# A hybrid attention, retention and expert layer on one core: stored operand loaded earlier, one interleave re-weighted, gate tiles double-buffered

## The chip, the cores and the metric

The kernel runs on 1 core of one Trainium2 chip. The metric is device time in microseconds; lower is better. Engines are named as the profile names them: PE (matrix multiply), PEld (its weight load), DVE (vector), ACT (activation), POOL (here it only issues indirect gathers) and SP (it issues the other DMAs).

## The reference

One decoder layer on 1024 tokens of width 1024, with 16 meta tokens ahead of them:

```
hn = rmsnorm(h);  z = hn @ w_in
y_a = attention(z) @ w_mla_out          # 8 heads, causal, low-rank q and kv
y_r = retention(z) @ w_ret_out          # 8 heads, chunks of 128, group norm, silu gate
h  += (sigmoid(za) * y_a + sigmoid(zr) * y_r) @ w_mix_out
x   = rmsnorm(h);  q = x @ w_peer_q     # 8 heads
top-16 of 128 keys on each of two sides -> top-16 of the 256 pairs, softmax gates
out = h + sum over the 128 chosen experts of gate * gelu(x . peer_u[e]) * peer_v[e]
```

There are 16384 experts. All is float32; the kernel makes its large products from three products of a high and a low part.

## The kernel before

**Token groups.** The 8 blocks of 128 tokens form three groups: blocks 0 to 2, 3 and 4, and 5 to 7. Each group passes through `latents`, `mix` (retention and attention), `merge` and `output`. `interleave(parts, counts)` steps two generators so that each reaches its count at the same time. `STEPS[1]` holds the counts for the merge of group n beside the latents of group n+1: (112, 90) for the second merge and the third latents. A merge has 112 steps: per column block two products of 4 + 2 and 4 + 4 steps. The third latents, counted through the yields of the code, have 98. What is left of one part when the other is done runs alone.

**Two ways for the experts.** Group 0 gathers its chosen rows (`gathered`, a background task: POOL gathers a row, DVE multiplies it at L1082 or adds it at L1087, 2 x 128 rows a block). The other five blocks (640 tokens) go through all experts densely in `dense`: 128 expert rows `e`, each with 128 experts. For each `e`, `scores(e)` loads 512 KB of `peer_ut` into a `raw` tile (ring of 3), splits it on ACT (`whi`) and DVE (`wlo`), multiplies it with the 256 stored tokens of group 1 (`x_hi`, `x_lo`) and the 384 of group 2 (`xT_hi`, `xT_lo`), and applies gelu into `gl`.

**The stored operand.** Group 1's normed tokens are written to DRAM (`xT_d`) by its `output`. At the start of `dense` they are loaded back through four `raw` tiles and copied by ACT into `x_hi` and `x_lo` (L1142), behind everything of the last `output`.

**Order in `dense`.** First 48 expert rows are scored and parked in DRAM (`gl_d`) while the gate matrix is built in the background: 20 stores of 2 MB into `gate_d`. Then `finish(0)`, five loads of `y`, and 16 groups of 8 expert rows, in the order `es`. A group is two quads of four rows; a quad is either parked (its `gl` comes back by a DMA of 320 KB, without PE work) or scored anew. Eight groups are scored then parked, four are scored twice, four parked then scored (these are the 4th, 8th, 12th and 16th). For each row `weights(e)` multiplies `gl` with its gates from the tile `gt` on DVE (L1209), and splits the product into `c_hi` (ACT) and `c_lo` (DVE). Then PE multiplies the eight products with `peer_vt` into `zacc`, in two halves, and DVE adds them to `y` (L1242).

**The gate tile.** `gt` holds the gates of one quad: one DMA of 1280 KB at every fourth row (L1208), into a pool with `GTB = 1` buffer:

```
if e % 4 == 0:
    gt[0] = vp.tile([P, nt, 4, TS], F32, name="gt", bufs=GTB)
    nc.sync.dma_start(gt[0], gate_d[...])
V.tensor_tensor(gl, gt[0][:, :, e % 4], gl, OP.mult)
```

Each load can start only when the multiplications of the quad before have read the buffer.

**What sets the order.** Each engine, and each DMA queue, takes its instructions in a fixed order that the tile framework makes from the program; a waiting instruction holds those behind it. Buffers are rings: a tile waits for the last reader of the tile whose place it takes. Background gathers are paced by the weight pieces that the main work consumes.

Of the kernel before, what the change touches and what calls it, by code (L numbers as in the profile page):

```python
# [12 lines left out]
F32 = mybir.dt.float32  # L13
# [29 lines left out]
RING = 3  # L43
ROWS = 4
SPLIT = 3
GTB = 1
DELAY = 8.0
STEPS = (((86, 72), (116, 64), (116, 144)), ((112, 90), (112, 90), (112,)), (80, 50))
HEAD = 20
BUBBLE = 12  # L50
LEAVE = ((6, 6, 3), (0, 1, 1))
# [92 lines left out]
def hybrid_layer(ctx: ExitStack, tc: tile.TileContext, out, a, dbg=None):  # L144
# [7 lines left out]
    ps = ctx.enter_context(tc.tile_pool(name="ps", bufs=2, space=PSUM))  # L152
    dram = ctx.enter_context(tc.tile_pool(name="dram", bufs=1, space=DRAM))

    gat = ctx.enter_context(tc.tile_pool(name="gat", bufs=1, side="right"))


# [90 lines left out]
        T.matmul(o, st[1], mv[0], start=False, stop=last)  # L248

    def square_sum(src, acc):  # L250
        junk = work.tile([P, TW], F32, name="zt").bitcast(BF16)
        S.activation(junk[:, :src.shape[-1]], src, AF.Square, accum_out=acc)

    def norm_scale(tiles, name):
# [61 lines left out]
    def group(g):  # L316
# [273 lines left out]
        def retention(hp):  # L590
# [45 lines left out]
            def add_state(i):  # L636
                pst = tr()
                for s in range(2):
                    T.matmul(pst[64 * s:64 * s + 64, 0:P], qn[:, i, 128 + 64 * s:128 + 64 * s + 64],
                             vr[:, i, P * s:P * s + P], start=True, stop=True)  # L640
                new = work.tile([P, P], F32, name=f"state{hp}")
                if hp in state:
                    V.tensor_tensor(new, pst[:, 0:P], state[hp], OP.add)
                else:
                    V.tensor_copy(new, pst[:, 0:P])
                state[hp] = new
# [179 lines left out]
        def merge():  # L826
            mg = own.mg
            for c in range(KD):
                for s, src in enumerate((own.oTs, own.yTs)):
                    pz = zacc()  # L830
                    for j, w in enumerate(split_pieces(a["w_z"][2 * c + s], KD, P)):
                        mm3(pz[:, 0, :W], w, [t[:, j, :W] for t in own.hn], j == 0, j == KD - 1)
                        if j % 2:
                            yield
                    n = len(src)
                    for j, w in enumerate(split_pieces(a["w_ret" if s else "w_mla"][c], n, P)):
                        mm3(pz[:, 1, :W], w, src[j], j == 0, j == n - 1)
                        if j % 2:
                            yield
                    th = work.tile([P, TW], F32, name="zt")[:, :W]  # L840
                    S.activation(th, pz[:, 0, :W], AF.Tanh, scale=0.5)
                    V.scalar_tensor_tensor(th if s else mg[:, c], th, 1.0, pz[:, 1, :W], op0=OP.add, op1=OP.mult)
                    if s:
                        V.tensor_tensor(mg[:, c], mg[:, c], th, OP.add)


        def output():
# [20 lines left out]
            if not last:  # L868
                if g >= NGROUP:
                    ktp = ctx.enter_context(tc.tile_pool(name=f"kt{g}", bufs=1, side="right", reuse_waits="tile"))  # L870
                fcs, fc = pool("fc", "right")
                scs = [pool(f"sc{i}_", "right") for i in reversed(range(nbk))][::-1]
            xps, xp = pool("xp", "right")
            xT = [xp.tile([P, KD, W], F32R, name=n) for n in ("xT_hi", "xT_lo")]
            hps, hp_ = pool("h2", "right")
# [215 lines left out]
        nc.sync.dma_start(out[P * b:P * b + P], acc[0])  # L1091


    def gate_matrix(i, kt, gT, p):

        stage = {}

        def products(t8, pairs):
            t0 = t8 // TS * TS
            if t8 == t0:  # L1100
                stage[0] = p.tile([P, P, TS], F32, name="stage", bufs=2)
            pg = zacc()
            oa, ob = pairs
            for t in range(8):
                T.matmul(pg[:, t // 4, P * (t % 4):P * (t % 4) + P], oa[:, t // 2, :, t % 2], ob[:, t // 2, :, t % 2],
                         start=True, stop=True)
            S.activation(stage[0][:, :, t8 - t0:t8 - t0 + 8].rearrange("p e (q t) -> p e q t", q=2),
                         pg.rearrange("p q (t e) -> p e q t", t=4), AF.Copy)
            if t8 == t0 + TS - 8:
                nc.sync.dma_start(gate_d[(P * i + t0) // TS], stage[0].rearrange("p e t -> p (e t)"))  # L1110

        pending = None
        for t8 in range(0, P, 8):
            at = lambda t: t.rearrange("p (q r) -> p q r", r=2).unsqueeze(2).to_broadcast([P, 4, P, 2])
            eq = [p.tile([P, 4, P, 2], BF16, name=f"eq{n}", bufs=2) for n in range(2)]
            for n in range(2):
                V.tensor_tensor(eq[n], iota_2.unsqueeze(1).to_broadcast([P, 4, P, 2]), at(kt[:, n, t8:t8 + 8]), OP.is_equal)
            pairs = [p.tile([P, 4, P, 2], F32, name=n, bufs=2) for n in ("oa", "ob")]
            S.activation(pairs[0], eq[0], AF.Copy)
            V.tensor_tensor(pairs[1], eq[1], at(gT[:, t8:t8 + 8]), OP.mult)  # L1120
            if pending:
                products(*pending)
            pending = (t8, pairs)
            yield 1.7
        products(*pending)

    def dense(xT):
        nt = DT // TS
        pacing["rates"] = RATES[3]
        last = GROUPS[-1]  # L1130
        segments = [(xT, len(last) * P)]
        xdp = ctx.enter_context(tc.tile_pool(name="xd", bufs=1, side="right", reuse_waits="tile"))
        for g, blocks in enumerate(GROUPS[NGROUP:-1]):
            w = P * len(blocks)
            t = [xdp.tile([P, KD, w], F32R, name=f"x_{n}{g}") for n in ("hi", "lo")]
            per = 1024 // w
            for dst, src in zip(t, xT_d[g]):
                for j in range(0, KD, per):
                    n = min(per, KD - j)
                    raw = wp.tile([P, 1024], F32, name="raw", bufs=RING)  # L1140
                    nc.sync.dma_start(raw[:, :n * w].rearrange("p (j c) -> p j c", j=n), src[:, j:j + n])
                    S.activation(dst[:, j:j + n].rearrange("p j c -> p (j c)"), raw[:, :n * w], AF.Copy)  # L1142
            segments.insert(g, (t, w))
        starts = [sum(w for _, w in segments[:k]) for k in range(len(segments))]
        order = list(range(len(segments)))
        ups, up = ExitStack(), None
# [14 lines left out]
        def routes():  # L1161

            kts, ktp = open_pool("ktl", "right")
            fcs, fc = open_pool("fcd", "right")
            n = len(last)
            top = top_tiles(n, fc)
            for h in range(H):
                first_top16(h, top, key_scores(queries(h, xT, n, fc), n))
                yield 1.85 * n
            for i, b in enumerate(last):  # L1170
                found = yield from choose(b, *top[i], fc, ktp)
                routed.append(found)
            fcs.close()
            pacing["rates"] = RATES[4]
            gms, gm = open_pool("gm")
            for i, (kt, gT) in enumerate(routed):
                yield from gate_matrix(i, kt, gT, gm)
            gms.close()
            kts.close()

# [11 lines left out]
        for b in range(NGATH, NBLK):  # L1192
            ys.append(vp.tile([P, D], F32, name=f"y{b}"))
            nc.sync.dma_start(ys[-1], h2_d[b])
        gt = {}

        def activations(e):
            if e >= AHEAD:
# [5 lines left out]
        def weights(e, gl):  # L1204

            if e % 4 == 0:
                gt[0] = vp.tile([P, nt, 4, TS], F32, name="gt", bufs=GTB)
                nc.sync.dma_start(gt[0], gate_d[:, :, TS * e:TS * e + 4 * TS].rearrange("n p (e t) -> p n e t", e=4))  # L1208
            V.tensor_tensor(gl.rearrange("p (n t) -> p n t", t=TS), gt[0][:, :, e % 4],  # L1209
                            gl.rearrange("p (n t) -> p n t", t=TS), OP.mult)  # L1210
            hi = vp.tile([P, DT], F32R, name="c_hi", bufs=CB)
            lo = vp.tile([P, DT], F32R, name="c_lo", bufs=CB)
            split(hi, lo, gl)
            return hi, lo


        es = [4 * n + k for n in sorted(range(P // 4), key=lambda n: (n + 0.5) / AHEAD if 4 * n < AHEAD else
                                        (n + 0.5 - AHEAD / 4) / (P - AHEAD)) for k in range(4)]
        for e0 in range(0, P, GE):
            group = es[e0:e0 + GE]  # L1220
            ne = len(group)
# [43 lines left out]
    iota = load_const("iota", a["c_iota"], [P, P])  # L1265
    iota_i = const.tile([P, 16, 2 * H], BF16, name="iota_i")
    V.tensor_copy(iota_i, iota[:, 0:16].unsqueeze(2).to_broadcast([P, 16, 2 * H]))
    iota_2 = const.tile([P, P, 2], BF16, name="iota_2")
    V.tensor_copy(iota_2, iota.unsqueeze(2).to_broadcast([P, P, 2]))
    gqr = load_const("gqr", bcast(a["g_qk"], 32, 64), [P, 32])  # L1270
    gkr = load_const("gkr", bcast(a["g_qk"], 32, 96 + 64), [P, 32])
    gqk = const.tile([P, 2], F32, name="gqk")
# [16 lines left out]
    for n, now in enumerate(groups):  # L1289
# [4 lines left out]
        now.open_merge(following)  # L1294
        interleave([now.merge()] + ([following.latents()] if following else []), STEPS[1][n])
        rest = now.output()
    dense(rest)
    finish(1)

# [17 lines left out]
```

## Time and profile before

| | |
|---|---|
| median of 3 runs | 3574.49 us (3563.3 to 3585.4) |
| profiled execution | 3571.28 us, span 3569.5 us |
| PE busy | 3322.8 us (93%) |
| DVE busy | 2687.7 us (75%) |
| ACT busy | 1268.1 us (36%) |
| mean granted TensorE clock | 0.968 |
| DMA | 837.12 MB, mean 235 GB/s |

The span is that of the profiled execution; its own time is 1.78 us more, and 3.2 us under the median. In the time rows the profile gives start and duration in microseconds, then the engine, line and operation, and in brackets how long the engine sat idle before and what released it. The granted clock is a share of 2.4 GHz; it is 1.00 or 0.50 (1.2 GHz), and values between are means over a stretch.

### The profile page before, as it was taken

The page shows a single profiled execution, that of the slowest core. Times are in us where ns is not written, and L with a number is a line of the kernel's source. Part 1 is how long each engine was busy: PE and PEld are TensorE (multiplying, and loading weights), DVE is VectorE, ACT ScalarE, POOL GpSimd, SP SyncE. Part 2 cuts the span into 40 slices and gives each one's busy share as a digit, 9 for nine tenths or more (in the row PEclk, how much of TensorE's full clock was granted, in tenths as well). Part 3 has the DMA queues.
Part 4 walks back from the last instruction along what each step waited for, and adds up shares of the span by engine and source line. Part 5 has one row for each costly group of instructions (what it writes and reads, how often), then busy time and mean ns, then how long its engine had stood idle before and what let it go on. Part 6 is the DMA issues. An engine that isn't in the chain of part 4 may idle for free.

```text
span 3569.5 us, 53608 instructions
## 1 busy us (share of the span) xinstructions
PE 3322.8 (93%) x20376; PEld 3022.3 (85%) x20376; DVE 2687.7 (75%) x5659; ACT 1268.1 (36%) x2097; POOL 1090.4 (31%) x772
## 2 busy tenths in 40 slices
PE   8999989989789998999999799999999999999999
PEld 7888988788767898999999788888788778887788
DVE  5645469898796676798988578777778777877776
ACT  3445334544445533234566222222222222222221
POOL 0000000112011122013434445454445454554454
PEclk9999999999899999999999899999999999999999
DMA  3322353557654377456777888888889888988886
GB/s 129 121 78 94 133 193 113 167 201 253 215 156 139 135 239 254 152 177 238 284 289 295 305 289 305 306 308 301 287 284 321 288 291 290 322 307 288 286 300 246
DMA packets 329251, 837.12 MB, mean 235 GB/s; under 512 B 45713, under 2 KB 140689, under 8 KB 326177
## 3 DMA queue, kind: packets, MB, share of 16 engines
q1 hardware_dynamic: 218400, 431.00, 35.4%
q0 software_dynamic: 110592, 402.70, 32.0%
q8 instruction: 160, 2.62, 0.3%
q14 instruction: 99, 0.80, 0.1%
HBM read 755.16 MB, written 78.43 MB: 234 GB/s over the span
## 4 chain that ended last, share of the span: by engine, by line
PE 49%; issue 17%; DMA 13%; DVE 11%; POOL 6%; ACT 3%; POOLq 0%; SPq 0%; DVEq 0%; ACTq 0%
PE zacc L246 10%; PE zacc L248 10%; PE zacc L247 10%; DMA row<-in_peer_v_dram,eidx 7%; POOL row L1065 6%; PE tr L246 4%; PE tr L247 4%; PE tr L248 4%; DMA gt<-gate_d 3%; DVE wlo L219 2%; PE tr L765 2%; PE sc L729 1%; DVE acc L1087 1%; ACT whi L218 1%; DMA row<-in_peer_u_dram,eidx 1%
## 5 line engine op out<-in xcount | busy, mean ns | idle before, releaser
L1065 POOL DMA_INDIRECT row<-in_peer_u_dram,eidx x384 | 486.3, 1266 | 1731.5 <-DVE row L1082 839.9
L218 ACT ACTIVATE whi<-raw 128x1024 fp32r<-128x1024 f32 (+2 forms) x508 | 520.7, 1026 | 1274.3 <-PE zacc L248 643.5
L219 DVE TENSOR_TENSOR wlo<-raw,whi 128x1024 fp32r<-128x1024 f32 (+2 forms) x508 | 599.5, 1181 | 369.6 <-ACT whi L218 368.7
L1065 POOL DMA_INDIRECT row<-in_peer_v_dram,eidx x384 | 603.9, 1573 | 718.5 <-DVE acc L1087 605.4
L246 PE MATMUL zacc<-whi,c_hi 128*128 128x512 f32 x1280 | 509.1, 398 | 57.0 <-ACT c_hi L218 45.9
L1087 DVE SCALAR_TENSOR_TENSOR acc<-row,dots,acc 128x1024 f32<-128x1024 f32 x384 | 482.0, 1278 | 91.0 <-DMA row<-in_peer_v_dram,eidx 90.2
L248 PE MATMUL zacc<-whi,c_lo 128*128 128x512 f32 x1280 | 506.8, 396 | 2.9 <-DVE c_lo L219 2.9
L247 PE MATMUL zacc<-wlo,c_hi 128*128 128x512 f32 x1280 | 506.3, 396 | 0.0
L1082 DVE SCALAR_TENSOR_TENSOR row<-row,xn 128x1024 f32<-128x1024 f32 x384 | 463.2, 1218 | 54.7 <-DMA row<-in_peer_u_dram,eidx 54.3
L246 PE MATMUL tr<-xT_hi,whi 128*128 128x384 f32 (+1 forms) x1216 | 416.3, 342 | 40.5 <-ACT gl L1158 39.3
L247 PE MATMUL tr<-xT_lo,whi 128*128 128x384 f32 (+1 forms) x1216 | 411.9, 339 | 0.0
L248 PE MATMUL tr<-xT_hi,wlo 128*128 128x384 f32 (+1 forms) x1216 | 411.7, 339 | 0.0
L246 PEld LDWEIGHTS zacc<-whi,c_hi 128*128 128x128 f32 x1280 | 245.4, 192 | 115.2 <-ACT c_hi L218 49.3
L246 PE MATMUL tr<-x_hi,whi 128*128 128x256 f32 x1024 | 295.9, 289 | 12.7 <-ACT whi L218 10.2
L248 PEld LDWEIGHTS zacc<-whi,c_lo 128*128 128x128 f32 x1280 | 244.7, 191 | 60.0 <-DVE c_lo L219 8.6
L247 PE MATMUL tr<-x_lo,whi 128*128 128x256 f32 x1024 | 290.2, 283 | 0.0
L248 PE MATMUL tr<-x_hi,wlo 128*128 128x256 f32 x1024 | 290.1, 283 | 0.0
L247 PEld LDWEIGHTS zacc<-wlo,c_hi 128*128 128x128 f32 x1280 | 245.3, 192 | 50.7
L246 PEld LDWEIGHTS tr<-xT_hi,whi 128*128 128x128 f32 x1216 | 233.6, 192 | 43.2 <-ACT gl L1158 40.8
L246 PE MATMUL zacc<-whi,hn_hi 128*128 128x256 f32 x832 | 250.8, 301 | 3.8 <-ACT pT L780 1.3
L247 PE MATMUL zacc<-wlo,hn_hi 128*128 128x256 f32 x832 | 238.9, 287 | 1.4 <-DVE wlo L219 1.4
L248 PE MATMUL zacc<-whi,hn_lo 128*128 128x256 f32 x832 | 238.1, 286 | 0.0
(286 smaller groups left out, 6728.8 us busy)
## 6 DMA issues: line engine op xcount, KB each, us to landing
raw<-in_peer_ut_dram SPq DMA_DIRECT2D x128, 512.0 KB, 5.5
raw<-in_peer_vt_dram SPq DMA_DIRECT2D x128, 512.0 KB, 6.2
gate_d<-stage SPq DMA_DIRECT2D x20, 2048.0 KB, 9.1
gt<-gate_d SPq DMA_DIRECT2D x32, 1280.0 KB, 14.6
raw<-in_w_nat_dram SPq DMA_DIRECT2D x72, 512.0 KB, 3.5
raw<-in_w_z_dram SPq DMA_DIRECT2D x48, 512.0 KB, 3.3
gl_d<-gl SPq DMA_DIRECT2D x48, 320.0 KB, 2.9
gl<-gl_d SPq DMA_DIRECT2D x48, 320.0 KB, 6.4
```

The lines of the kernel that those rows point to most:

```text
L218: S.activation(hi, src, AF.Copy)
L219: V.tensor_tensor(lo, src, hi.bitcast(F32), OP.subtract)
L246: T.matmul(o, st[0], mv[0], start=first, stop=False)
L247: T.matmul(o, st[0], mv[1], start=False, stop=False)
L248: T.matmul(o, st[1], mv[0], start=False, stop=last)
L729: T.matmul(sc[:, c, 0:w], qh, kT[0:96, k0:k0 + w], start=True, stop=c < nch - 1)
L765: T.matmul(oo, vh[:, c + k], pT[:, k], start=False, stop=c + k == b)
L1065: G.indirect_dma_start(out=row, out_offset=None, in_=table, in_offset=bass.IndirectOffsetOnAxis(ap=eidx[:, k:k + 1], axis=0))
L1082: op = V.scalar_tensor_tensor(row, row, 1.0, xn, op0=OP.mult, op1=OP.mult, accum_out=dots[:, k:k + 1])
L1087: op = V.scalar_tensor_tensor(acc[k % 2], row, dots[:, k:k + 1], acc[k % 2], op0=OP.mult, op1=OP.add)
```

## The change

Four things. The stored operand is loaded and copied when the last group's `output` opens, ahead of its `w_mix` loads, by the new function `stored_tokens`, whose loop stood in `dense` before. The counts of the second merge beside the third latents become (112, 100). `gt` has two buffers; `gate_tile` issues the first load ahead of the group loop and each further one a quad ahead. To make room, `iota_2` moves from the constants into the gate-matrix pool, and the tiles `zt` and `state` into a pool `mw` that is closed ahead of `dense`.

```diff
-GTB = 1
+GTB = 2
-STEPS = (((86, 72), (116, 64), (116, 144)), ((112, 90), (112, 90), (112,)), (80, 50))
+STEPS = (((86, 72), (116, 64), (116, 144)), ((112, 90), (112, 100), (112,)), (80, 50))
...
+    mixers = ExitStack()
+    mw = mixers.enter_context(tc.tile_pool(name="mw", bufs=2))
...
-        junk = work.tile([P, TW], F32, name="zt").bitcast(BF16)
+        junk = mw.tile([P, TW], F32, name="zt").bitcast(BF16)
...
-                new = work.tile([P, P], F32, name=f"state{hp}")
+                new = mw.tile([P, P], F32, name=f"state{hp}")
...
-                    th = work.tile([P, TW], F32, name="zt")[:, :W]
+                    th = mw.tile([P, TW], F32, name="zt")[:, :W]
...
     def output():
...
+            if last:
+                segments.extend(stored_tokens())
             xps, xp = pool("xp", "right")
...
+    segments = []
+
+    def stored_tokens():
+        xdp = ctx.enter_context(tc.tile_pool(name="xd", bufs=1, side="right", reuse_waits="tile"))
+        for g, blocks in enumerate(GROUPS[NGROUP:-1]):
+            w = P * len(blocks)
+            t = [xdp.tile([P, KD, w], F32R, name=f"x_{n}{g}") for n in ("hi", "lo")]
+            per = 1024 // w
+            for dst, src in zip(t, xT_d[g]):
+                for j in range(0, KD, per):
+                    n = min(per, KD - j)
+                    raw = wp.tile([P, 1024], F32, name="raw", bufs=RING)
+                    nc.sync.dma_start(raw[:, :n * w].rearrange("p (j c) -> p j c", j=n), src[:, j:j + n])
+                    S.activation(dst[:, j:j + n].rearrange("p j c -> p (j c)"), raw[:, :n * w], AF.Copy)
+            yield t, w
...
     def dense(xT):
-        segments = [(xT, len(last) * P)]
...
-            segments.insert(g, (t, w))
+        segments.append((xT, len(last) * P))
...
             gms, gm = open_pool("gm")
+            iota_2 = gm.tile([P, P, 2], BF16, name="iota_2")
+            V.tensor_copy(iota_2, iota.unsqueeze(2).to_broadcast([P, P, 2]))
...
-        gt = {}
+        gts = deque()
+
+        def gate_tile(e):
+            gts.append(vp.tile([P, nt, 4, TS], F32, name="gt", bufs=GTB))
+            nc.sync.dma_start(gts[-1], gate_d[:, :, TS * e:TS * e + 4 * TS].rearrange("n p (e t) -> p n e t", e=4))
...
             if e % 4 == 0:
-                gt[0] = vp.tile([P, nt, 4, TS], F32, name="gt", bufs=GTB)
-                nc.sync.dma_start(gt[0], gate_d[:, :, TS * e:TS * e + 4 * TS].rearrange("n p (e t) -> p n e t", e=4))
-            V.tensor_tensor(gl.rearrange("p (n t) -> p n t", t=TS), gt[0][:, :, e % 4],
+                if e != es[0]:
+                    gts.popleft()
+                if e != es[-4]:
+                    gate_tile(es[es.index(e) + 4])
+            V.tensor_tensor(gl.rearrange("p (n t) -> p n t", t=TS), gts[0][:, :, e % 4],
...
+        gate_tile(es[0])
         for e0 in range(0, P, GE):
...
+    mixers.close()
     dense(rest)
```

## Rows read from the trace of the kernel before

**Rows 1.** The page, busy time of each engine, its share and instructions.
```profile
PE 3322.8 (93%) x20376; PEld 3022.3 (85%) x20376; DVE 2687.7 (75%) x5659; ACT 1268.1 (36%) x2097; POOL 1090.4 (31%) x772
```

**Rows 2.** Stretches of the group loop: length, busy times, clock, DMA share, GB/s.
```profile
1986.20:3563.50 1577.30, 1475.85 (x7682) 1305.58 (x7680) 1204.12 (x1447) 366.25 (x497) 767.14 (x558) 0.97 0.85 296
2312.30:2395.00 82.70, 82.70 (x435) 73.26 (x434) 66.89 (x102) 18.41 (x24) 43.43 (x34) 1.00 0.91 323
2312.30:2340.40 28.10, 28.10 (x193) 28.06 (x192) 25.82 (x40) 8.79 (x14) 16.27 (x12) 1.00 0.93 334
...
2394.90:2486.70 91.80, 85.05 (x435) 74.30 (x434) 70.38 (x105) 21.57 (x29) 44.20 (x34) 0.96 0.85 293
2581.80:2701.70 119.90, 112.78 (x627) 102.86 (x626) 91.45 (x90) 30.99 (x44) 60.79 (x43) 0.99 0.84 287
```

**Rows 3.** PE's waits in the group loop: us in total, times, longest.
```profile
PE zacc L246 <- ACT c_hi L218: 45.9, 8, 7.6
PE tr L246 <- ACT gl L1158: 41.4, 6, 20.1
PE zacc L246 <- DVE y L1242: 9.9, 10, 2.1
```

**Rows 4.** DVE's waits in the group loop.
```profile
DVE gl L1209 <- DMA gt<-gate_d: 107.4, 17, 9.5
DVE acc L1087 <- DMA row<-in_peer_v_dram,eidx: 78.2, 44, 5.9
```

**Rows 5.** Timeline of one stall, in the fifth group.
```profile
2426.08 0.37 SPq L1208 DMA_DIRECT2D gt<-gate_d  x1
2427.96 7.97 SPq L1201 DMA_DIRECT2D gl<-gl_d  x1
...
2441.66 2.30 DVE L1209 TENSOR_TENSOR gl<-gt,gl 128x640 f32<-128x640 f32 x3 [8.19 <-DMA gt<-gate_d]
2442.52 2.21 ACT L218 ACTIVATE c_hi<-gl 128x640 fp32r<-128x640 f32 x3 [11.45 <-DVE gl L1209]
...
2443.31 0.79 PE L246 MATMUL zacc<-whi,c_hi 128*128 128x512 f32 x1 [6.53 <-ACT c_hi L218]
```

**Rows 6.** DMA issues of 2424 to 2440 us: count, KB each, us to landing.
```profile
gl<-gl_d SPq DMA_DIRECT2D x1, 320.0 KB, 14.4
```

**Rows 7.** DMA issues of 2340 to 2365 us, in the fourth group.
```profile
gt<-gate_d SPq DMA_DIRECT2D x1, 1280.0 KB, 15.1
```

**Rows 8.** Stretches of 2 us behind that stall.
```profile
2442.00:2444.00 2.00, 0.69 (x2) 0.50 (x2) 2.00 (x4) 1.48 (x3) 0.00 (x0) 0.50 0.08 33
...
2448.00:2450.00 2.00, 2.00 (x10) 1.68 (x9) 2.00 (x4) 0.74 (x1) 1.70 (x2) 1.00 0.07 10
```

**Rows 9.** Timeline of the first gate tile.
```profile
1990.14 1.75 SPq L1194 DMA_DIRECT2D y<-h_d  x3
...
1994.39 0.42 SPq L1208 DMA_DIRECT2D gt<-gate_d  x1
...
2023.34 0.69 PE L246 MATMUL tr<-xT_hi,whi 128*128 128x384 f32 x1 [20.06 <-ACT gl L1158]
```

**Rows 10.** Timeline of the entry into `dense`.
```profile
1419.91 1.99 ACT L1142 ACTIVATE x_hi<-raw 128x1024 fp32r<-128x1024 f32 x2
1421.80 1.04 ACT L1142 ACTIVATE x_lo<-raw 128x1024 fp32r<-128x1024 f32 x1
...
1421.93 1.28 SPq L1150 DMA_DIRECT2D raw<-in_peer_ut_dram  x2
...
1429.56 0.58 PE L246 MATMUL tr<-x_hi,whi 128*128 128x256 f32 x1 [10.18 <-ACT whi L218]
```

**Rows 11.** Timeline of the last `output`'s entry.
```profile
1356.07 15.98 SPq L235 DMA_DIRECT2D raw<-in_w_mix_dram  x5
1372.73 1.46 SPq L878 DMA_DIRECT2D h<-in_x_dram  x3
...
1373.60 0.28 PE L246 MATMUL zacc<-whi,mT_hi 128*128 128x256 f32 x1
```

**Rows 12.** PE's wait at the end of the second merge, of 880 to 1000 us.
```profile
PE tr L482 <- DVE nat L556: 13.2, 3, 5.9
```

**Rows 13.** Timeline of ACT there.
```profile
894.59 0.65 ACT L542 ACTIVATE sq<-zacc 128x576 f32<-128x576 f32 x1 [6.71 <-DVE nat L556]
...
904.20 0.65 ACT L542 ACTIVATE sq<-zacc 128x576 f32<-128x576 f32 x1 [6.04 <-DVE nat L556]
```

**Rows 14.** The `iota_2` copy, duration ns min/median/max.
```profile
L1269 DVE CAST iota<-iota x1: 285/285/285, 13.8 to 13.8; 128x256 bf16<-128x256 f32 x1
```

More of the change, by code (lines that the diff above doesn't have):

```diff
@@ L1091, in gathered, with gate_matrix @@
         nc.sync.dma_start(out[P * b:P * b + P], acc[0])
-    def gate_matrix(i, kt, gT, p):
+    segments = []
[12 more added lines that the diff above has]
+            yield t, w
+    def gate_matrix(i, kt, gT, iota_2, p):
         stage = {}
@@ L1130, in dense @@
         last = GROUPS[-1]
-        segments = [(xT, len(last) * P)]
[L1132 to L1142, printed above, removed]
-            segments.insert(g, (t, w))
+        segments.append((xT, len(last) * P))
         starts = [sum(w for _, w in segments[:k]) for k in range(len(segments))]
@@ L1175, in routes @@
             gms, gm = open_pool("gm")
+            iota_2 = gm.tile([P, P, 2], BF16, name="iota_2")
+            V.tensor_copy(iota_2, iota.unsqueeze(2).to_broadcast([P, P, 2]))
             for i, (kt, gT) in enumerate(routed):
-                yield from gate_matrix(i, kt, gT, gm)
+                yield from gate_matrix(i, kt, gT, iota_2, gm)
             gms.close()
@@ L1267, in hybrid_layer @@
     V.tensor_copy(iota_i, iota[:, 0:16].unsqueeze(2).to_broadcast([P, 16, 2 * H]))
-    iota_2 = const.tile([P, P, 2], BF16, name="iota_2")
-    V.tensor_copy(iota_2, iota.unsqueeze(2).to_broadcast([P, P, 2]))
     gqr = load_const("gqr", bcast(a["g_qk"], 32, 64), [P, 32])
```

## The prediction

> **What bounds the kernel now.** I read the page first: PE is busy 93% of the span, DVE 75%, and nothing else is near [rows 1]. So time can be won only where PE stands still or runs slowly. The table of stretches shows where that is: the largest part lies in the 16 groups at the end (the first row of [rows 2], from the first product of the first scored row), the rest at the joints between the token groups. The fourth group (parked quad first) takes 82.7 us with PE busy throughout and the clock at 1.00. The fifth does the same work, only with the parked quad second, and takes 91.8 us, 85.05 of them busy, at 0.96. The 8th, 12th and 16th run like the fourth, so the trace holds its own control: four groups in which the gate tile is never late, and twelve in which something is.
>
> What is late is read from the waits, back from PE. In the group loop PE waits 45.9 us for `c_hi`, 41.4 us for gelu to free a PSUM tile (20.1 us of it once) and 9.9 us for the adds to `y` [rows 3]. DVE waits 107.4 us, in 17 waits, for `gt` [rows 4]. The timeline joins them [rows 5]: SP issues the load at 2426.08, DVE sits 8.19 us idle until it has landed at 2441.66, ACT makes `c_hi` at 2442.52 and PE goes on at 2443.31 after 6.53 us. Where both quads are scored, ACT stands in front of `c_hi` with PE's gelu queued behind it, and PE waits for the PSUM tile instead. A stall also costs on the way out: the clock is 0.50 at 2442 and 1.00 again only from 2448 [rows 8], so some 4 us of work run at half speed and 2 us are lost beside the wait.
>
> **The second gate tile.** First the floor of the loop. A group with a parked quad takes 82.7 us; four more scored rows cost 28.1 us [rows 2]. Twelve groups of 82.7 and four of 110.8 make 992 + 443 = 1435.6 us. The stretch lasts 1577.3 us [rows 2], so 141.7 us lie over the floor. Check from PE's side: 101.5 us idle (1577.3 less 1475.85) and about 40 us of busy time that the low clock stretches.
>
> Of this the first tile keeps its part. It is issued at 1994.39, directly behind the five `y` loads that begin at 1990.14, and PE goes on at 2023.34 after 20.06 us [rows 9]. The change puts `gate_tile(es[0])` behind the same `y` loads, so I see nothing that brings it forward: 20.1 us of wait and about 3 us of slow clock stay. The bounds, at the 334 GB/s of the scoring stretch [rows 2], are 8 us better (should it pass the 2.6 MB of `y`) and 4 us worse (the second tile's 1.3 MB ahead of it). 118.6 us are left that can go.
>
> For the 31 later tiles the load of quad q+1 now takes the place in SP's order where quad q's stood: both wait for the last multiplication of quad q-1. The DMA stream stays what it was, one tile further on. The lead grows by a whole quad, at least 28.1 us where it is scored [rows 2], and a half-group of `zacc` work more in most cases. In the fourth group the gate tile landed 15.1 us after its issue with gathers running beside it [rows 7], so the lead covers it, and the 107.4 us of DVE waits shrink to the first tile's 9.
>
> Then I ask what is late next. In the eight groups with the parked quad second, the third `gl` of that quad is queued behind a gate tile: issued at 2427.96, it landed 14.4 us later, at 2442.4 [rows 6]. It needs one multiplication and one split (0.8 and 0.7 us, a third of the groups of three in [rows 5]), so `c_hi` is there at 2443.9. PE stood from 2436.78 (2443.31 less 6.53) and would come to this row one weight piece later (an eighth of 82.7 - 28.1, 6.8 us): at 2443.6. The fourth `gl` waits for a buffer that the first one frees and comes some 2 us behind. What do these groups lose now? The seventh group, both quads scored, takes 119.9 us where 110.8 is the floor [rows 2]: 9.1 over, 36 for the four of its kind, which leaves 82 of the 118.6 for the eight, 10 each. Between 0 and all 10 may stay; the row puts the miss at 0.3 us for the third `gl` and 2 for the fourth, so I take 2: 8 x 2 = 16 us stay.
>
> The adds to `y` keep half of their 9.9 us: they are DVE queued behind gathered rows, for which it waits 78.2 us in all [rows 4], and the fourth group has none of it. That is 5 us. The tile brings 118.6 - 16 - 5 = 97 us, between 36 (all eight stay as late as now) and 118.
>
> The Trainium skill has a rule against this, in "DMA: Bandwidth & Descriptors", section "Queues, rings and completion order": each DMA engine takes turns between the queue rows that have work. A stalled DVE frees no gather buffers, so by the rule a tile loaded beside running gathers would take up to twice as long. The row of the fourth group, 15.1 us, speaks against a large effect; twice that would still lie inside the lead of a scored quad, and only the `gl` queued behind it would suffer, which is the first rival below, 3508.
>
> **The stored operand.** Now ACT copies the four pieces from 1419.91 on, the first `peer_ut` pieces are issued behind them at 1421.93, and PE starts at 1429.56 after 10.18 us [rows 10]. With the four loads and copies (1.05 us each) gone from there, the `raw` ring lets `peer_ut` come in during the norm, and the split is ready when the transposes end. What is late next is the last transposed block itself, under 1 us. The clock is low here already through the norm's own wait, so no gain is added for it. The four loads and copies go ahead of the `w_mix` loads. The ring has three places, so `w_mix` can no longer be fetched from 1356 on [rows 11]: its first piece waits for the second copy, which waits for the merge's attention operand to be read out of the space that `x_hi` takes. By the row PE wants that piece at 1373.60; I get it split between 1373 and 1376. The `h` loads (1372.73) move a tile lower and may hold SP until the last `mg` is read. Bounds of this cost: 0 and the 10 us won. I take 3. Net gain 7 us.
>
> **The interleave.** The latents have 98 steps, so at a count of 90 eight or nine run alone behind the merge, and there PE waits 13.2 us in three waits for DVE's `nat` [rows 12]. With 100 the merge's last ten steps, 60 products of 256 columns, lie between them: 7 us, at 28.1 us for four rows of 24 x 640 columns [rows 2]. But the query units form a chain of their own: ACT's square for the next unit waits 6 to 7 us for the last `nat` [rows 13], about 9.6 us a unit, and this chain runs on whatever PE does; it only starts up to 7 us earlier, and shares DVE with the merge's splits. I take 5 us, between 0 and 12.
>
> **Answers with one term.** `iota_2` costs 0.3 us on DVE [rows 14], once, in a background task. The moved `zt` and `state` tiles are last read in the norm of the last `output`, ahead of the first `gl` that can take their place; nothing.
>
> **The sum.** 97 + 7 + 5 = 109 us off the profiled 3571.28 gives 3462.3. That execution lies 3.2 us under the median of 3574.49, a tenth of a per cent, which I leave in the range. About 1% is what a measurement of this kernel tells from no change.
>
> **Rivals.**
> *The parked rows take the place.* If `gl` behind the tile lands later than I take it, because DMA no longer pauses, the eight groups keep most of their wait. They carry 82 us; with three quarters of that kept 62 stay in place of 16, and the time is 3508. For it speaks the 14.4 us [rows 6]; against it that the miss there is 0.3 us, not 7.
> *Transfers become the bound.* The loop moves 296 GB/s over 1577.3 us, 467 MB. In 1480 us that is 315 GB/s; the fourth group held 323 with PE at full speed and its scoring part 334 [rows 2], so there is room for one group, not shown for 16 in a row. If 305 is what lasts, the loop takes 1531 us, 51 more, and the time is 3513. (The Trainium skill, same page, Specifications, gives about 358 GB/s from HBM for a core; by that alone it would not bind.)
> *The change does not do what it says:* the second buffer comes free as late as the first, should its place overlap something read late. Then only 12 us remain: 3559.
> *Slower.* SP takes its queue in order. If a tile's issue now stands ahead of weight pieces that could go, and waits for its buffer, PE runs dry. Each such wait costs its length and 2 us of clock; with 31 loads the sign turns where PE loses more than about 3.5 us at each (109 / 31). At 5 us with 2 of clock it would be 3571 + 31 x 7 - 109 = 3679. Against it: the same wait stands at the same place now, and weight pieces are not among PE's long waits [rows 3].
>
> **Chances.** My forecast, 3430 to 3500: 0.73. Parked rows 0.09, transfers 0.09: both near 3510. Not as said 0.05. Slower 0.04. Range 3428 to 3514: its lower end takes 118 us for the tile, 10 and 12 for the rest and leaves a little for the first tile; the upper end takes in the two rivals near 3510. Faster by over 1%: 0.92; within 1%: 0.05; slower: 0.03.
>
> **What would show it.** Waits of DVE for `gt`: one, of about 9 us, at the first tile. Groups of scored then parked quads at 83 to 86 us, all-scored ones at 111 to 113. PE's 10.18 us at the entry gone, `x_hi` copied before 1375, and at most a few us of wait in front of `w_mix`. PE's wait for `nat` halved. The forecast is wrong if PE's waits for `c_hi` stay above 25 us, if the clock in the loop stays under 0.99, or if waits for rows grow on DVE until `y` is late in every group.

## The result

The changed kernel takes 3533.28 us (median of 4 runs) beside 3573.11 for the kernel before: ratio 0.9882, 95% interval 0.9841 to 0.9924. Faster, but by 40 us where 109 were forecast, and above the upper end of the range, 3514. The profiled execution lasts 3531.8 us (span) against 3569.5 before; these 37.7 us are taken apart here.

The page after, busy time of the engines:
```profile
PE 3313.8 (94%) x20376; PEld 3016.2 (85%) x20376; DVE 2686.0 (76%) x5659; ACT 1263.5 (36%) x2097; POOL 1073.8 (30%) x772
```
Stretches after, with the columns of [rows 2]: the group loop, then the fourth, fifth and seventh group.
```profile
1978.60:3525.80 1547.20, 1466.69 (x7682) 1300.31 (x7680) 1202.43 (x1446) 363.02 (x497) 757.38 (x558) 0.97 0.87 301
2296.00:2379.30 83.30, 82.91 (x434) 73.20 (x433) 67.51 (x103) 18.29 (x24) 43.97 (x34) 1.00 0.92 322
2379.20:2470.80 91.60, 85.00 (x435) 74.70 (x434) 70.36 (x105) 21.22 (x29) 41.99 (x34) 0.96 0.88 299
2562.70:2678.20 115.50, 112.66 (x627) 102.45 (x626) 92.34 (x90) 30.87 (x44) 60.37 (x42) 0.99 0.88 300
```
The loop is 30.1 us shorter, not 97. The fifth group, scored quad first, takes 91.6 us where it took 91.8 [rows 2]; its stall has only changed its name. PE's waits in the loop:
```profile
PE zacc L248 <- DVE y L1260: 54.4, 12, 9.1
PE tr L248 <- ACT gl L1167: 17.1, 4, 15.2
PE zacc L250 <- DVE c_lo L221: 5.8, 6, 2.5
PE zacc L248 <- ACT c_hi L220: 3.1, 3, 1.8
```
and DVE's:
```profile
DVE gl L1226 <- DMA gl<-gl_d: 69.8, 31, 5.4
DVE acc L1091 <- DMA row<-in_peer_v_dram,eidx: 62.2, 36, 5.0
DVE row L1086 <- DMA row<-in_peer_u_dram,eidx: 52.1, 35, 5.1
...
DVE gl L1226 <- DMA gt<-gate_d: 5.6, 1, 5.6
```
Two more of DVE's waits before, which [rows 4] leaves out:
```profile
DVE row L1082 <- DMA row<-in_peer_u_dram,eidx: 54.3, 47, 3.6
...
DVE gl L1209 <- DMA gl<-gl_d: 3.1, 4, 1.7
```
Beside [rows 3, 4]: `gt` fell from 107.4 us to the one wait at the first tile and `c_hi` from 45.9 to 3.1, as said. But the adds to `y` rose from 9.9 us to 54.4, in 12 stalls, one in every group but the 4th, 8th, 12th and 16th. Behind ten of them PE runs for some us at the lower clock, so the loop's mean clock is 0.97 as before. On DVE the wait for parked rows (`gl_d`) rose from 3.1 us to 69.8; the waits for gathered rows did not grow (132.5 us before, 114.3 now). Timeline of such a stall, in the fifth group:
```profile
2413.21 0.37 SPq L1210 DMA_DIRECT2D gt<-gate_d  x1
...
2425.21 0.38 SPq L1210 DMA_DIRECT2D gt<-gate_d  x1
...
2436.41 1.23 DVE L1086 SCALAR_TENSOR_TENSOR row<-row,xn 128x1024 f32<-128x1024 f32 x1 [4.35 <-DMA row<-in_peer_u_dram,eidx]
...
2437.56 1.22 DVE L221 TENSOR_TENSOR wlo<-raw,whi 128x1024 fp32r<-128x1024 f32 x1
...
2438.71 1.23 DVE L1086 SCALAR_TENSOR_TENSOR row<-row,xn 128x1024 f32<-128x1024 f32 x1
...
2439.86 1.28 DVE L1260 TENSOR_TENSOR y<-zacc,y 128x512 f32<-128x512 f32 x2
...
2441.28 0.77 PE L248 MATMUL zacc<-whi,c_hi 128*128 128x512 f32 x1 [6.60 <-DVE y L1260]
```
PE ends the first half at 2434.70 and can begin the second only when DVE has emptied the accumulator. DVE stands at a gathered row that has not landed; then it does that row, a weight piece and one more row, and only then the first adds. Behind the stall the clock is 0.50:
```profile
2443.00:2445.00 2.00, 2.00 (x6) 1.52 (x6) 2.00 (x3) 0.00 (x0) 0.49 (x1) 0.50 0.93 303
```
Added up over the timelines of the twelve stalls, DVE is idle for a row in 9.3 of the 54.4 us. It spends 20.7 us on rows, 8.6 on weight pieces and 13.6 on the adds themselves. So late data holds `y` mostly through the work that it leaves standing in DVE's queue.

From the group's first `zacc` product to the stall the DMA engines had no pause (share 0.98):
```profile
2407.30:2434.70 27.40, 27.39 (x121) 22.32 (x119) 19.35 (x29) 7.88 (x10) 10.69 (x9) 1.00 0.98 326
```
But full engines alone make no stall: the fourth and the eighth group show 0.98 and 0.99 in the same half and have none. What sets the groups apart is a wait of DVE in this half. In the fifth group, its largest for a DMA:
```profile
DVE gl L1226 <- DMA gl<-gl_d: 5.1, 3, 2.3
```
and in the fourth, its only one:
```profile
DVE row L1086 <- DMA row<-in_peer_u_dram,eidx: 5.3, 3, 2.9
```
DVE's 69.8 us for `gl_d` lie in the first halves of the twelve groups that stall, 2.5 to 11.6 us in each; the other four have none of it, though three of them wait 4.4 to 5.3 us for rows. So the waits for parked and for gathered rows add up on DVE ahead of the adds. No run takes the parked rows away alone, so their share is read from the traces and not shown by an experiment.

Outside the loop the first scored row starts 2.9 us later (1432.47 against 1429.56 [rows 10]), and the stage of parked scores takes 531.0 us where it took 541.5, which I had not foreseen. -30.1 - 10.5 + 2.9 = -37.7. The 2.9 us are one execution against one: with the same parts ahead of it, the first score lies between 1422.5 and 1434.2 in the other traces. That stage before:
```profile
1429.50:1971.00 541.50, 528.63 (x3727) 523.92 (x3728) 474.50 (x1059) 264.11 (x333) 180.59 (x85) 0.99 0.66 239
```
and after:
```profile
1432.40:1963.40 531.00, 525.20 (x3728) 521.15 (x3728) 464.17 (x1046) 260.21 (x329) 176.02 (x84) 0.99 0.67 240
```
The entry after, in timeline rows of ACT, PE and DVE:
```profile
1371.22 1.06 ACT L1112 ACTIVATE x_lo<-raw 128x1024 fp32r<-128x1024 f32 x1 [2.95 <-DMA raw<-xT_lo]
...
1376.17 0.58 PE L248 MATMUL zacc<-whi,mT_hi 128*128 128x256 f32 x1 [5.03 <-ACT whi L220]
...
1418.10 0.69 DVE L1138 TENSOR_TENSOR eq<-iota,kt 128x1024 bf16<-128x1024 bf16 x1
...
1426.01 2.48 DVE L906 SCALAR_TENSOR_TENSOR xnt<-h,r_f,g_ffn 128x1024 f32<-128x1024 f32 x2
```
The 10.18 us of [rows 10] are gone. In their place PE waits 5.03 us for the first `w_mix` piece, behind the stored copies, and 12.44 in place of 5.56 for the last normalised tile: the gate matrix's comparisons (`eq`) now stand on DVE between the steps of that norm. Before, the first of them came at 1632.8.

### The profile page after: what moved, and what is told of

The parts are those of the page before. It is cut to its first block, busy times and chain, and to the rows that moved or that the text cites. A ratio compares the mean times of both kernels' runs of the same rounds, so it can differ in the third digit from the quotient of the medians.

```text
span 3531.8 us, 53573 instructions
## 1 busy us (share of the span) xinstructions
PE 3313.8 (94%) x20376; PEld 3016.2 (85%) x20376; DVE 2686.0 (76%) x5659; ACT 1263.5 (36%) x2097; POOL 1073.8 (30%) x772
## 4 chain that ended last, share of the span: by engine, by line
issue 26%; PE 20%; POOL 12%; DVE 8%; DMA 8%; ACT 1%; POOLq 0%; SPq 0%; DVEq 0%; ACTq 0%
POOL row L1069 12%; DMA row<-in_peer_v_dram,eidx 6%; PE zacc L248 4%; PE zacc L250 4%; PE zacc L249 4%; PE tr L248 2%; DVE wlo L221 2%; PE tr L249 2%; PE tr L250 2%; PE tr L767 1%; DVE acc L1091 1%; DMA row<-in_peer_u_dram,eidx 1%; PE sc L731 1%; DVE row L1086 1%; DMA gl<-gl_d 1%
## 5 line engine op out<-in xcount | busy, mean ns | idle before, releaser
L1069 POOL DMA_INDIRECT row<-in_peer_v_dram,eidx x384 | 589.1, 1534 | 698.2 <-DVE acc L1091 583.0
L248 PE MATMUL zacc<-whi,c_hi 128*128 128x512 f32 x1280 | 510.2, 399 | 57.6 <-DVE y L1260 54.4
```

The source lines that it names most:

```text
L248: T.matmul(o, st[0], mv[0], start=first, stop=False)
L1069: G.indirect_dma_start(out=row, out_offset=None, in_=table, in_offset=bass.IndirectOffsetOnAxis(ap=eidx[:, k:k + 1], axis=0))
```

## The experiments

**The parts alone.** Each kernel is the one before with one part of the diff: `GTB = 2` with the look-ahead and the moved pools, `stored_tokens()` alone, `(112, 100)` alone.

> The gate tiles alone: two buffers, loaded a quad ahead, with the moved tiles that make room; stored operand and interleave as before. Theory A (the loss sits in the group loop: adds to y are held on DVE behind late gathered rows): the loop looks as in the changed kernel, PE waits about 54 us for y, and the kernel gains about 30 us, near 3541. It should also carry the early eq work of the gate matrix inside the last norm (PE waits about 12 us there instead of 5.6). Rival B (the other two parts ate a gain that the tiles alone would give): 3480 or less.

> The early load of the stored operand alone. Theory A: the 10 us wait at the entry of the dense stage goes, a wait of about 5 us for w_mix comes at the start of the last output, and the wait for the norm stays at 5.6 us, since the early eq work belongs to the gate tiles' part: about 5 us gained, 3566. Rival B (the early load itself delays the norm): PE waits about 12 us for xnt, and 3574 or more.

> The count 100 in place of 90 alone. Expected by the changed kernel's trace: 2 to 3 us gained, inside the noise, near 3569; PE's waits for nat spread over four places and add up to about 7 us instead of 13. Rival: 6 us or more gained, and the later parts took it back.

Measured: 3546.29 (ratio 0.9916, 0.9888 to 0.9944), 3568.88 (0.9991, 0.997 to 1.0011) and 3564.78 (0.9986, 0.9968 to 1.0003). The gate tile alone brings some 25 to 30 us and already has the new wait for `y` (62.2 us); it also brings the early `eq` (11.5 us of wait for the norm). The other two cannot be told from nothing by their times. With the stored operand alone `w_mix` costs PE 3.9 us; the interleave cuts its wait for `nat` from 13.2 us [rows 12] to 5.3 (6.1 in the full change).

**Two tiles close together.** In the fifth group the two tiles are issued 12 us apart; before it was some 23.
```
-                if e != es[-4]:
-                    gate_tile(es[es.index(e) + 4])
+                n = es.index(e)
+                if n == 0 or n % GE and n + 4 < P:
+                    gate_tile(es[n + 4])
 ...  # behind the first half's adds to y
+                if not s and e0 + GE + 4 < P:
+                    gate_tile(es[e0 + GE + 4], ys[ND - 1][:, 0:1])
```

> The changed kernel, with each group's second prefetch (the tile for the second quad of the next group) held until the first half's adds to y, by a copy of one column from y into the tile ahead of its load; so one gate tile loads in each half of a group. Theory A (transfers: both tiles within 12 us of the first half make gathered rows late, and y waits behind them): PE's wait for y falls from 54 to under 25 us and the time to 3495 to 3510. Rival C (DVE has too much to do in the first half, whatever the transfers): the wait for y stays near 54 us and the time within 5 us of the changed kernel, 3533.

Measured 3519.69 (0.9845, 0.9819 to 0.987): some 14 us less than the change by the medians, but the single runs of both lie between 3519 and 3540 and the intervals overlap, so the gain is not shown. In its profiled run, the slowest of its five at 3539.70, `y` keeps 50.5 us in 12 waits, only more evenly spread. So the bunching alone is not what makes `y` late.

**Rows, or DVE's work?** One kernel sets `RATES[5]` to `(0.0, 0.0)`, so that no row runs in the loop; the other does DVE's work on rows in `[:, 0:P]` only.

> The changed kernel, but in the group loop no gathered row is paced; the some 550 rows that the loop carries come behind it, so the whole is far longer (estimate 4200 to 4500 us) and only the loop's own length is read (changed kernel: 1547 us; worked-out floor 1436). Theory (gathered rows in DVE's order hold the adds to y, by their transfers or by their work): PE's wait for y falls from 54 us to under 8, DVE's wait for gl_d from 70 us to under 15, the loop takes 1440 to 1470 us, the first gate tile's 15 us among it. Rival (the loads of parked gl and the two gate tiles alone make the lateness, rows only add to it): y keeps over 25 us and the loop stays above 1500.

> The changed kernel, but each gathered row, still fetched whole, is multiplied and added in its first 128 columns only (the rest of the retrieved part is left out): the transfers stay, DVE's work on rows falls from some 690 us in the loop to under 150. Theory T (late transfers hold DVE's queue): PE's wait for y stays above 30 us, the loop above 1510 us, and DVE's waits for rows grow. Theory W (DVE has too much to do between two half boundaries, 1202 us of work against a floor of 1436): the wait for y falls under 12 us and the loop to 1470 or less.

Measured 4496.26 and 3579.05 (one run each). Without rows, the stretches of the loop and of the rows behind it, and PE's only wait in the loop:
```profile
1960.00:3411.30 1451.30, 1449.15 (x7781) 1298.35 (x7779) 562.38 (x626) 366.60 (x500) 5.00 (x5) 1.00 0.37 121
3411.30:4490.00 1078.70, 0.02 (x1) 0.00 (x0) 713.64 (x826) 0.62 (x2) 689.30 (x558) 0.50 0.81 275
```
```profile
PE tr L248 <- ACT gl L1167: 2.1, 1, 2.1
```
The stretch begins some 14 us ahead of the first scored row, in the end of the stage before, so the loop itself takes some 1437 us. That is the floor of the prediction: clock 1.00, no wait for `y`, and 2.1 us at the first gate tile. I had thought that this tile was held by the `y` loads, but these stand ahead of it here too. DVE still waits for parked `gl`, where under 15 us were expected, without harm to anyone:
```profile
DVE gl L1226 <- DMA gl<-gl_d: 85.5, 32, 6.3
```
With the rows' transfers kept and their work cut:
```profile
1960.00:3571.00 1611.00, 1491.14 (x7738) 1316.58 (x7736) 697.92 (x1447) 363.23 (x500) 554.63 (x558) 0.96 0.84 291
```
```profile
PE zacc L248 <- DVE y L1260: 72.2, 13, 9.8
PE zacc L248 <- ACT c_hi L220: 23.8, 10, 4.0
```
DVE is busy 698 us instead of 1202, and `y` waits longer than ever; in 46.8 of these 72.2 us DVE is idle for a row. So less work on DVE alone does not free `y`: then the rows themselves are what it waits for. In the changed kernel, where DVE works through most of the stalls, late data and the work on it act together; this run does not part them. Why this is slower than the change stays open: the order of DVE's instructions changed with the shorter work too.

**Early comparisons held back.** One more line makes `iota_2` wait for the last routing result:
```
+            V.tensor_copy(iota_2[:, 0, 0:1], routed[-1][1][:, 0:1])
```

> The changed kernel with one more tiny copy into iota_2 that reads the last routing result, so that the comparisons of the gate matrix cannot begin ahead of it. Theory: these comparisons stand between the steps of the last norm on DVE and delay the entry; PE's wait for the normalised transposes falls from 12.4 us to 5 to 7, and the kernel gains 5 to 8 us (3525 to 3528 beside 3533). Rival: the work is only moved into the stage of parked scores, where the changed kernel was 10 us shorter than the one before; the entry gains 6 us, that stage loses as much, and the total stays within 3 us.

Measured 3535.55 (0.9902, 0.988 to 0.9924): nothing gained. PE's waits at the entry, and the stage of parked scores:
```profile
PE tr L275 <- DVE xnt L906: 6.8, 2, 6.5
```
```profile
1420.60:1962.00 541.40, 527.78 (x3728) 523.34 (x3729) 471.35 (x1058) 262.07 (x330) 174.88 (x84) 0.99 0.65 236
```
The entry is won back (6.5 for 12.4 us; the first score comes at 1420.65), and the stage takes 541.4 us as before the change. The first `eq` is back at 1622.5. The same DVE work is paid in one place or the other.

**The order on DVE.** Rows of a half are put behind the adds of the half before, none with the last weight piece:
```
+                    pacing["piece"] = (1.3 * ND * 4 / 3) if e < ne - 2 else 0.0
 ...
+                    added[0] = V.tensor_tensor(y, acc[i // 2][:, i % 2], y, OP.add)
 ...  # each row operation behind added[0]
```

> The changed kernel with the gathered rows of a half ordered on DVE behind the five adds to y of the half before, and none emitted with the half's last weight piece; as many rows, transfers and multiplications as before. Theory (a late row just ahead of the adds is what holds y, because the adds have only some 4 us of slack while weight pieces are split two pieces, 13 us, ahead): y falls from 54 us to under 20, zacc stages to 55 to 58 us, and the kernel comes to 3485 to 3505. Rival (DVE and transfers are short over the whole loop, whatever the order): the waits come back at the split weights or at c_hi, and the time stays within 10 us of 3533.

Measured 3578.03 (1.0019, 1.0003 to 1.0035). PE's waits in its loop:
```profile
PE tr L248 <- ACT gl L1172: 45.7, 16, 16.9
PE zacc L249 <- DVE wlo L221: 37.7, 10, 6.7
PE zacc L248 <- DVE y L1267: 14.2, 5, 3.8
PE zacc L248 <- ACT c_hi L220: 12.0, 5, 3.9
```
`y` fell as I said, and late data stopped other things instead. The rival had the kind right: the order chooses who waits. It had the size wrong: the largest wait came at gelu, which it did not name, and the time is 45 us above the change, where it allowed 10.

**When and how far ahead rows and tiles are asked for.** First, in each mixed group the parked quad stands first (on the change, then on the kernel before):
```
+        es = [e for g in range(0, P, GE) for e in sorted(es[g:g + GE], key=lambda e: (e >= AHEAD, es.index(e)))]
```

> The changed kernel with the two quads of each mixed group exchanged where the scored one stood first, so that all twelve mixed groups have the order of the 4th, 8th, 12th and 16th; loads, products and rows are the same in number. Theory (the transfers have room over a group, but a parked quad's gl, the gate tiles and the gathered rows fall together where the parked quad comes second, and there a row is late): the twelve mixed groups take 82.7 to 84 us like those four, y falls from 54 us to under 25, the kernel comes to 3470 to 3500. Rival (the transfers are short over the whole loop: 29 MB a group, at the some 343 GB/s of the busy engines 85 us; the four groups were only helped by the slack that the late ones leave): the four lose their advantage, the lateness spreads, the time stays at 3520 to 3540.

> The kernel before (one gate tile, loaded when the one ahead is used up), with the same exchange of quads. Theory: the eight groups that ran 91 us run nearer to 83 without a second tile, DVE's wait for gt falls from 107 us to under 45, and the kernel gains 40 to 75 us (3500 to 3530), as much as the whole change or more. Rival: in front of a scored quad the one tile is late too, or rows become late as in the changed kernel, and it gains under 35 us (3540 or more).

Then one more row buffer (`MORE = 1`), taken from `vp` while the loop runs; and two more, with one gate tile as before:
```
+            ring["n"] += 1
+            if ring["more"] and ring["n"] % (ROWS + MORE) < MORE:
+                row = ring["more"].tile([P, D], F32, name="row", bufs=MORE)
 ...
-            while todo and len(rows) < ROWS - 1:
+            while todo and len(rows) < ROWS - 1 + (MORE if ring["more"] else 0):
```

> The changed kernel with one more buffer for gathered rows inside the group loop (four gathers under way in place of three); its place comes from constants that end with the last output stage. Theory (a row is late by up to 5 us because three gathers ahead cover some 7.6 us only, when other loads crowd in): DVE's waits for rows fall from 114 us to under 60, y from 54 to under 30, and the kernel comes to 3500 to 3520. Rival (the engines are the limit, more requests only take from gl, weights and the gate tiles): rows gain, gl_d and the pieces lose, the time stays within 10 us of 3533 or grows.

> The changed kernel with one gate tile again, loaded when the one ahead is used up, and two more row buffers (8 KB of the 10 KB of the second tile) in the loop. Theory (lateness of rows is the larger part): gt waits come back at some 107 us on DVE, rows nearly vanish (under 40 us), and the time lies between 3520 and 3550. Rival (the gate tile is what counts, row depth is nothing): 3560 or more, as before with only the small parts won.

Measured: parked first 3502.44 (0.982, 0.9791 to 0.9848); on the kernel before 3527.60 (0.9887, 0.9856 to 0.9917), as much as the whole change, though `gt` falls only to 81.0 us there, where under 45 was expected; five rows 3495.52 (0.9792, 0.9763 to 0.982); six rows with one tile 3544.27 (0.9941, 0.9922 to 0.9959). Parked first takes `y` to 33.7 us, where under 25 was expected: seven of the twelve mixed groups have their `zacc` stage at the floor of 54.6 to 54.9 us, where four had. But the fourth and the eighth have lost it, so a part of the rival holds, and the first group's wait grows from 15 to 30 us. With five rows DVE's waits in the loop are
```profile
DVE gl L1234 <- DMA gl<-gl_d: 79.5, 36, 5.5
DVE acc L1098 <- DMA row<-in_peer_v_dram,eidx: 27.3, 15, 8.3
DVE row L1093 <- DMA row<-in_peer_u_dram,eidx: 13.6, 13, 2.5
```
41 us for rows instead of 114, and `y` 30.0 instead of 54.4. With six rows and one tile row waits nearly vanish (21.3 us) and `gt` is back at 121.1: the rows' lateness and the tile's can be had one without the other.

**Together.** Five rows, and parked first from the second group on; then the same order with six rows and one tile; then with the second tile held as above.

> The changed kernel with one more row buffer in the loop and, from the second group on, the parked quad first in every mixed group (the first group keeps its order, since with the parked quad first its wait for the first gate tile grew from 15 to 30 us). Theory (both repairs act on the same late transfers, so they overlap but each still removes what the other leaves): y under 15 us, 3465 to 3485. Rival (one cause, fully cured by either as far as it can be): the time stays at 3488 to 3500, as with five rows alone.

> As the run before, but with one gate tile loaded when the one ahead is used up, and two more row buffers in place of the second tile. Theory (with the parked quad first the single tile is needed late in most groups, so the second tile is worth little then): 3480 to 3510. Rival (the gate tile ahead stays worth its 30 to 50 us whatever the order): 3520 or more.

> Five rows, the parked quad first from the second group on, and the next group's second gate tile asked for only when the first half's adds to y are done (the run named held before this one lost most adds to y in the edit and is read as a kernel without them). Theory (two tiles within a few us are a burst that delays the rows): 5 to 15 us under the 3463 of five rows and parked first. Rival (four gathers under way cover the burst): within 4 us of it, or slower, since the second quad's tile now comes later.

Measured 3463.28 (0.9689, 0.9663 to 0.9715), 3507.99 (0.9808, 0.9766 to 0.9849) and 3470.71 (0.9723, 0.9699 to 0.9747). The first, its loop (again from 14 us ahead of the first scored row, so some 1479 us) and PE's longest waits there:
```profile
1961.20:3453.90 1492.70, 1459.30 (x7775) 1303.24 (x7774) 1205.60 (x1450) 367.50 (x502) 769.71 (x563) 0.99 0.90 316
```
```profile
PE zacc L249 <- DVE y L1269: 18.5, 9, 4.8
PE tr L249 <- ACT gl L1174: 12.3, 1, 12.3
```
The repairs nearly add up (38 and 31 us alone, 70 together; alone, the order of quads also lost some 8 us in the first group, which kept its order here). `y` is at 18.5 us, where under 15 was expected. The second tile is still worth some 45 us there, and holding it back brings nothing more. An earlier try at the held one lost nine of the ten adds to `y` of each group in the edit; read as a loop nearly without them it took 3452.96 us. That is 10 us under the kernel without the hold and 18 under the one with it; its own hold stands ahead of the one add that is left, so it is the like of neither, and the adds can still cost 10 to 18 us there at most.

> Five rows, the parked quad first from the second group on, and the first gate tile issued ahead of the five y loads of 2.6 MB. Theory (the tile waits behind those loads; at 334 GB/s they take 8 us): PE's first wait falls from 15 to 7 to 10 us and the kernel gains 6 to 9 us on 3463. Rival (the first tile waits for the last writes of the gate matrix and for gathered rows, not for y): under 3 us.

Measured 3460.11 (0.9694, 0.9664 to 0.9724), no difference from 3463. Its trace shows that the edit did not do what it says: four `y` loads were still issued at 1985.31 and the tile at 1988.67. So it tells nothing on the rival; the run without rows does, where the tile behind the same loads kept PE 2.1 us.

## Why the prediction was wrong

**The second gate tile** was forecast at 97 us; the loop gave 30.1. Right were its removal of the `gt` waits, the floor of 1436 us (some 1437 without rows, 2.1 of it the first wait), the groups with the parked quad first (83.3 us), `c_hi`, and that SP's queue does no harm (it waits 106.6 us for the tile's place where it was 50.4, but PE waits for no weight piece). The step that failed is "The adds to `y` keep half of their 9.9 us [...] That is 5 us": 54.4 us. I priced the adds by the wait that they had while DVE's stall for `gt` stood ahead of them and stopped PE as well. With that stall gone PE reaches the half boundary some 7 us earlier in the mean (in the fifth group 55.3 us after the group's start, before 64.5), and DVE, which now waits for parked rows and gathered rows in turn, does not. I had asked what these waits cost PE directly, at `c_hi`, and not what they leave standing ahead of the adds. My reason for the small figure, that the fourth group has none of it, was their order's doing; turned round, seven of the twelve mixed groups ran without it, but the fourth and the eighth did not.

The terms: the loop was to take 1436 + 20.1 + 3 + 16 + 5 = 1480 us and took 1547. Of these 67 us, 49 are `y`, 28 the clock (busy 1466.69 is 31 over the floor, 3 were allowed), 11 `c_lo`, `c_hi` and small waits for gelu; 5 less came from the first tile (15.2 for 20.1), and the 16 for parked rows did not come where I put them (49 + 28 + 11 - 5 - 16 = 67).

**The rivals.** "Transfers become the bound" was nearest, 3513 with 305 GB/s; the loop ran at 301. But it was not a ceiling on the rate: the same bytes go at 316 GB/s with one more row buffer and another order of quads. What bound was how early rows and tiles are asked for. "The parked rows take the place" had half of it: they are late now, 69.8 us on DVE for 3.1, but PE meets it at `y` and not at `c_hi` (3.1 us). By themselves they do no harm: without gathered rows DVE waits 85.5 us for them, and PE only 2.1, at the first tile.

The rule of the Trainium skill weighed there ("DMA: Bandwidth & Descriptors", section "Queues, rings and completion order", engines take turns between rings with work) fits what happened to the gathers rather than the tile: DVE stood 4.35 us for a row with the engines 98% busy. No run here separates the turns from plain fullness, and two groups as full had no stall.

**The stored operand** was forecast to gain 7 us at the entry. The 10.18 us went, and `w_mix` cost 5.03 where I took 3. With the operand alone, one trace against one, PE's waits at the entry fall by some 4 us (10.2 gone, 3.9 and 0.7 for `w_mix`, 1.2 more for the norm and 0.7 for the last block come). What I missed is a dependence, not a size: the moves that make room for the second tile, `iota_2` among them, which I costed at 0.3 us "once, in a background task", let `eq` float forward by some 215 us, into the norm. It costs 6 us there and gave 10.5 back in the next stage; both vanish together when `iota_2` is held. Whether the copy or the moved pools set `eq` free, no run parts.

**The interleave**: 5 us forecast; the wait for `nat` fell by 7.1 and two others took some back (`h` 2.6 for 0.5, `mT_hi` 1.7). The next attention scores (`sc`) begin at 988.14 for 990.63. Over all traces, the fifteen kernels with the new count begin them at 976.7 to 989.1 (median 985.3) and the four with the old at 990.6 to 996.5 (median 991.2), so it is some 6 us. Right, though the run times alone cannot tell it from nothing.

## What to carry to other kernels

When a wait is taken from an engine that works in order, follow that engine's queue to the next items whose data comes by another path, ask how early that data was asked for, and add up what their waits leave standing ahead of the work that another engine needs; the price that this had behind the old wait is no measure. A kernel short of lead, not of bandwidth, shows it when one more buffer or another order of the same loads moves the time; one run without the suspected stream gives the floor. Moving an instruction's release can move work that you did not touch: compare whole stages, not the edited lines.

## What was not expected

The gathered rows alone, with nothing beside them but their DVE work, took 1.93 us each (558 in 1078.7 us) at 275 GB/s and a DMA share of 0.81, with three under way. And the transfers of the loop went faster, 316 GB/s for 301, when less was waited for, though no byte was taken out. Open stays whether holding the second tile alone gives anything: four of its five runs lie near 3519.5, and the profiled one, at 3539.70, shows nearly the same waits as the change.
